# A macaron encoder layer in split fp32: longer leads at three boundaries, and operand places on one offset

## The chip, the cores and the metric

One Trainium2 chip, one of its cores. The metric is device time of one execution in microseconds: 1952.46 us before the change (median of 3 runs, 1952.25 to 1954.24).

## The reference

One encoder layer on x of 256 tokens by 2048 channels, float32, with three blocks, each behind a norm that is modulated by nine vectors made from c:

```python
mod = silu(c) @ w_ada + b_ada            # 2048 -> 9 * 2048
h = rms_norm(x, ffn1_pre_g) * (1 + sc1) + sh1
f = (silu(h @ w_gate) * (h @ w_up)) @ w_down        # 2048 -> 5632 -> 2048
x = x + 0.5 * g1 * rms_norm(f, ffn1_post_g)
h = rms_norm(x, mix_pre_g) * (1 + sc2) + sh2
q, k, v, c_val, c_gate = split(h @ w_in)            # 2048 -> 5120
attn = 8 heads, rotary, three dilated windows
u = silu(layer_norm(depthwise_conv31(c_val * sigmoid(c_gate))))
x = x + g2 * rms_norm(concat(rms_norm(attn), rms_norm(u)) @ w_out, mix_post_g)
# then a second FFN like the first, with sh3, sc3, g3
```

## The kernel before

**Matmuls.** The 256 tokens are two halves t of 128 partitions. A product of a 128x128 block of the transposed activations (stationary) and 128x512 weights (moving) is computed from split operands: both sides are held as a rounded part (hi) and a rest (lo), and L316 to L318 add hi*hi, hi*lo and lo*hi into one PSUM bank per half. A Group (L294) is one 512-column block of a product over all its K tiles; it goes by chunks of CH = 2 K tiles. `wchunk` (L280) loads a chunk on the sync queue into one of 7 `raw` buffers, casts it on ACT to `hi` (L290) and subtracts on DVE to `lo` (L291); hi and lo have 4 buffers each. A chunk is 12 matmuls: 2 K tiles, 3 products, 2 halves. Six PSUM banks hold three groups.

**in_step** (L320) loads several chunks, then issues the products of half 0 for all of them, then those of half 1, then one `tick` for each. `group` (L329) takes `head` chunks in one step, then single chunks, then `tail` chunks in one step. With TAIL = 4 at the last group of a block, half 0 is complete 24 matmuls before half 1; with HEAD = 4 the next block begins with half 0 of four chunks.

**Boundaries.** `next_norm` (L409) follows a block: `post_add` of half 0 (norm of f, add to x, sum of squares), `pre_norm` (L360) of half 0 for the first JF = 4 K tiles, `post_add` of half 1, and the rest. `pre_norm` scales x by the norm (DVE), transposes two K tiles (TensorE), applies A and B of the modulation (ACT), and splits into hi and lo (ACT, DVE).

**Modulation.** `mod_sum` (L169) loads w_ada in half-MB blocks into the same `raw` buffers and sums it times silu(c) per partition on DVE (L191); `mod_cols` transposes the sums and adds them up over partitions on ACT. These run as lanes: generators that `tick` steps at a rate per chunk.

**Stages.** `ffn_start` (L465) computes the first six 512-column blocks of gate and up (12 groups) K stage by K stage, since the modulation of the next K tiles is still being made: STAGES1 has four stages of 4 K tiles, STAGES2 has 4, 6 and 6. At the start of the kernel all of stage 0's modulation (16 ada blocks, `first`, L550) precedes the first product. `begin2` (L568) opens FFN 2 with two groups in step. The lane of stage s + 1 is paced so that it ends two chunks before the stage does.

**Places.** Activations live in named places of the work pool (`slot`, L249): `ah`/`al` 0 to 5, `hh`/`hl` 0 to 3, `fs`, `gs`, `ac`; 4096 bytes per partition each, `ah5` and `al5` 4576 (SLOT = 4 * 286 elements). Within a pool tiles follow one another in the order of their first use. By the sizes of what stands before them, the hi/lo buffers start 64 bytes past a multiple of 256, and the places of h at a multiple of 256.

The order within an engine is set by a scheduler when the program is built; program order gives the priority.

Of the kernel before, what the change touches and what calls it, by code (L numbers as in the profile page):

```python
# [9 lines left out]
F32 = mybir.dt.float32  # L10
# [6 lines left out]
P = 128  # L17
# [15 lines left out]
CH = 2  # L33
MW = 1024

HEAD = 4
TAIL = 4  # L40
# [10 lines left out]

RAW = 7
HILO = 4
SLOT = 4 * (S + 2 * PAD)

STAGES1 = ((0, 4), (4, 8), (8, 12), (12, 16))
STAGES2 = ((0, 4), (4, 10), (10, 16))


@with_exitstack  # L60
def encoder_layer(ctx, tc, a, consts, out):
# [215 lines left out]
            return self.lo[k // 4][:, k % 4:k % 4 + n, :]  # L277


    def wchunk(w, r0, kt, cols, name):  # L280

        raw = wpool.tile([P, CH, BLK], F32, tag="raw", bufs=RAW, name=f"raw_{name}")
        hi = wpool.tile([P, CH, BLK], F32R, tag="hi", name=f"hi_{name}")
        lo = wpool.tile([P, CH, BLK], F32R, tag="lo", name=f"lo_{name}")
        r, h, l = raw[:, :kt, :], hi[:, :kt, :], lo[:, :kt, :]
        n = BLK // len(cols)
        for m, n0 in enumerate(cols):
            nc.sync.dma_start(r[:, :, m * n:(m + 1) * n],
                              w[r0:r0 + kt * P, n0:n0 + n].rearrange("(j p) n -> p j n", p=P))
        nc.scalar.copy(h, r)  # L290
        nc.vector.tensor_tensor(l, r, f32(h), op=ALU.subtract)  # L291
        return h, l

    class Group:  # L294
# [6 lines left out]
            self.first, self.last, self.kx = first, last, kx  # L301
            self.chunks = -(-nk // CH)

        def load(self, c):
            kt = min(CH, self.nk - c * CH)
            return wchunk(self.w, (self.k0 + c * CH) * P, kt, self.cols, f"{self.name}_{c}")

        def products(self, c, t, hl):
            ts = slice(t * P, (t + 1) * P)
# [10 lines left out]
    def in_step(work):  # L320

        hls = [g.load(c) for g, c in work]
# [6 lines left out]
    def group(*args, head=0, tail=0, **kw):  # L329

        g = Group(*args, **kw)
        head = min(head, g.chunks - tail)
        mid = range(head, g.chunks - tail)
        for cs in (range(head), *([c] for c in mid), range(g.chunks - tail, g.chunks)):
            in_step([(g, c) for c in cs])
# [72 lines left out]

    def next_norm(f, ssp, A, B, j1, i):  # L409


        hT = Parts(f"h{i}", "h", range(4))
        jh = min(HEAD * CH, j1)
        rs = [post_add(f, post_rstd(ssp, i, 0), i, 0)]
        pre_norm(hT, rs, A, B, 0, JF, i, 0, 1)
        rs.append(post_add(f, post_rstd(ssp, i, 1), i, 1))
        pre_norm(hT, rs, A, B, JF, jh, i, 0, 1)
        pre_norm(hT, rs, A, B, 0, jh, i, 1, 2)
        pre_norm(hT, rs, A, B, jh, j1, i)
        return hT, rs  # L420


    def act_out(aT, i, gs, pu, name):
# [26 lines left out]
    def ffn_down(f, aT, wd, ba, bb, th, G, ssp, i):  # L450
        for db in range(4):
            pd = mm_ps(f"pd{i}_{th}_{db}")
            group(pd, aT, wd, ba * 4, (bb - ba) * 4, db * BLK, f"d{i}_{th}_{db}",
                  tail=TAIL if th == 1 and db == 3 else 0)
            for t in range(NT):
# [4 lines left out]
                if th == 1:  # L460
                    post_block(f, ssp, G, t, db)

    ROUNDS = ((0, 6, (0, 1, 2, 3, 4, 5)), (6, 11, (0, 1, 2, 3, 5)))

# [78 lines left out]
    def ffn1_mods(s):  # L543
        return stage_mods(0, 1, "ffn1_pre_g", A1, B1, *STAGES1[s])
# [328 lines left out]
    drain(conv_entry)  # L873
    drain(mods)
    r2 = rc["conv"]
    for db in range(4):
        po = mm_ps(f"pc{db}")
        group(po, mT, w_out, 8, 8, db * BLK, f"oc{db}", kx=8, tail=TAIL if db == 3 else 0)
        for t in range(NT):
            nc.vector.scalar_tensor_tensor(f[db][:, t, :], po[t], r2[:, t:t + 1],  # L880
                                           f[db][:, t, :], op0=ALU.mult, op1=ALU.add)
            post_block(f, ssp, G2, t, db)


    hT, rs = next_norm(f, ssp, A3, B3, STAGES2[0][1], 3)
# [66 lines left out]
```

## Time and profile before

| | us |
|---|---|
| median of 3 runs | 1952.46 |
| profiled execution | 1953.91 |
| its span, first to last instruction | 1952.1 |
| TensorE busy | 1872.6 (96%) |
| DVE busy | 1474.1 (76%) |
| ACT busy | 928.3 (48%) |
| DMA queue q1, share of 16 engines | 76.1% |
| mean granted TensorE clock | 0.989 |

A row of a timeline has the start, the duration, the engine, the line, the operation with output<-inputs, the shape and a count (x8: eight merged), and in brackets the engine's idle time before it with what ended it. Matmuls overlap: the distance of starts is what one costs, not its duration. In a table of waits stand the total, the count and the longest. A window's row has each engine's busy time, then the granted clock, the DMA share and the rate.

### The profile page before, as it was taken

What the parts mean: (1) busy time and instruction counts of PE and PEld (TensorE: products, weight loads), DVE (VectorE), ACT (ScalarE), POOL (GpSimd) and SP (SyncE); (2) the same over time, 40 slices, a digit from 0 to 9 for tenths busy, and PEclk for the clock granted to TensorE, in tenths of its full rate; (3) what the DMA queues carried; (4) which work ended last, traced back from release to release, by engine and by line L of the source; (5) the groups of instructions that cost most, each with busy time, mean ns of one, the idle gap of its engine ahead of it and who ended that gap; (6) DMA issues with size and microseconds to landing.
All of it is one profiled execution on the core that took longest, in us unless ns stands there. A gap on an engine that the chain in (4) does not pass through costs nothing.

```text
span 1952.1 us, 23783 instructions
## 1 busy us (share of the span) xinstructions
PE 1872.6 (96%) x8358; PEld 1527.1 (78%) x8358; DVE 1474.1 (76%) x1824; ACT 928.3 (48%) x1428; POOL 66.0 (3%) x99
## 2 busy tenths in 40 slices
PE   2999999999999999899999988999999999999997
PEld 1888877888888888688888776687888888888886
DVE  6789999787777776689997777897786556545455
ACT  3554355444444444644456655534444443444442
POOL 2000000000000000000100000000000000000000
PEclk9999999999999999899999999999999999999999
DMA  9989978999999898357555767897777777666653
GB/s 344 310 297 311 323 253 283 348 340 328 314 321 316 317 318 292 109 184 224 173 165 161 239 214 258 301 341 254 226 247 244 244 253 248 195 185 191 206 191 101
DMA packets 250392, 496.29 MB, mean 254 GB/s; under 512 B 17209, under 2 KB 42625, under 8 KB 250272
## 3 DMA queue, kind: packets, MB, share of 16 engines
q1 hardware_dynamic: 247888, 491.38, 76.1%
q0 software_dynamic: 2208, 3.32, 0.5%
q8 instruction: 65, 1.06, 0.2%
q14 instruction: 55, 0.45, 0.1%
q10 hardware_dynamic: 176, 0.07, 0.0%
HBM read 492.58 MB, written 2.12 MB: 253 GB/s over the span
## 4 chain that ended last, share of the span: by engine, by line
PE 88%; DVE 5%; DMA 3%; ACT 2%; issue 2%; POOL 0%; DVEq 0%; POOLq 0%; ACTq 0%; SPq 0%
PE pd_t L318 8%; PE pd_t L317 8%; PE pd_t L316 8%; PE pg_t L317 8%; PE pg_t L318 8%; PE pg_t L316 8%; PE pu_t L318 8%; PE pu_t L317 8%; PE pu_t L316 7%; PE pc_t L316 2%; PE pc_t L318 2%; PE pc_t L317 2%; DVE acc L191 2%; DMA ada<-in_w_ada 1%; PE pa L384 1%
## 5 line engine op out<-in xcount | busy, mean ns | idle before, releaser
L191 DVE SCALAR_TENSOR_TENSOR acc<-ada,cact,acc 128x512 f32<-128x512 f32 (+2 forms) x448 | 384.9, 897 | 12.8 <-DMA acc<-in_b_ada 8.4
L291 DVE TENSOR_TENSOR lo_d<-raw_d,hi_d 128x1024 fp32r<-128x1024 f32 x176 | 215.3, 1225 | 157.6 <-ACT hi_d L290 156.9
L290 ACT CAST hi_d<-raw_d 128x1024 fp32r<-128x1024 f32 x176 | 185.2, 1052 | 261.2 <-PE pd_t L318 181.5
L290 ACT CAST hi_g<-raw_g 128x1024 fp32r<-128x1024 f32 x176 | 185.0, 1052 | 247.2 <-PE pg_t L318 121.0
L291 DVE TENSOR_TENSOR lo_g<-raw_g,hi_g 128x1024 fp32r<-128x1024 f32 x176 | 214.4, 1222 | 105.0 <-ACT hi_g L290 104.8
L291 DVE TENSOR_TENSOR lo_u<-raw_u,hi_u 128x1024 fp32r<-128x1024 f32 x176 | 213.9, 1222 | 104.7 <-ACT hi_u L290 104.4
L290 ACT CAST hi_u<-raw_u 128x1024 fp32r<-128x1024 f32 x176 | 184.8, 1052 | 214.0 <-PE pu_t L318 94.5
L318 PE MATMUL pd_t<-hi_d,a_0l 128*128 128x512 f32 x384 | 151.2, 394 | 0.0
L317 PE MATMUL pd_t<-lo_d,a_0h 128*128 128x512 f32 x384 | 150.5, 392 | 0.0
L316 PE MATMUL pd_t<-hi_d,a_0h 128*128 128x512 f32 x384 | 150.4, 392 | 0.0
L316 PE MATMUL pg_t<-hi_g,h3h 128*128 128x512 f32 x352 | 140.4, 401 | 5.3 <-ACT hi_g L290 4.2
L316 PE MATMUL pu_t<-hi_u,h3h 128*128 128x512 f32 x352 | 139.8, 400 | 2.9 <-ACT hi_u L290 2.9
L317 PE MATMUL pu_t<-lo_u,h3h 128*128 128x512 f32 x352 | 140.0, 398 | 1.7 <-DVE lo_u L291 1.6
L317 PE MATMUL pg_t<-lo_g,h3h 128*128 128x512 f32 x352 | 139.4, 396 | 1.7 <-DVE lo_g L291 1.7
L316 PE MATMUL pg_t<-hi_g,h1h 128*128 128x512 f32 x352 | 139.4, 398 | 1.0 <-ACT hi_g L290 1.0
L318 PE MATMUL pu_t<-hi_u,h3l 128*128 128x512 f32 x352 | 139.7, 397 | 0.0
L317 PE MATMUL pg_t<-lo_g,h1h 128*128 128x512 f32 x352 | 138.7, 394 | 0.8 <-DVE lo_g L291 0.8
L318 PE MATMUL pg_t<-hi_g,h3l 128*128 128x512 f32 x352 | 139.3, 396 | 0.0
L316 PE MATMUL pu_t<-hi_u,h1h 128*128 128x512 f32 x352 | 138.8, 396 | 0.0
L318 PE MATMUL pu_t<-hi_u,h1l 128*128 128x512 f32 x352 | 138.6, 394 | 0.0
L318 PE MATMUL pg_t<-hi_g,h1l 128*128 128x512 f32 x352 | 138.6, 395 | 0.0
L317 PE MATMUL pu_t<-lo_u,h1h 128*128 128x512 f32 x352 | 137.8, 392 | 0.1
(259 smaller groups left out, 3572.1 us busy)
## 6 DMA issues: line engine op xcount, KB each, us to landing
ada<-in_w_ada SPq DMA_DIRECT2D x288, 512.0 KB, 5.3
raw_g<-in_ffn_w_gate SPq DMA_DIRECT2D x176, 512.0 KB, 4.7
raw_u<-in_ffn_w_up SPq DMA_DIRECT2D x176, 512.0 KB, 4.7
raw_d<-in_ffn_w_down SPq DMA_DIRECT2D x176, 512.0 KB, 5.7
raw_c<-in_w_in SPq DMA_DIRECT2D x64, 256.0 KB, 3.1
raw_q<-in_w_in SPq DMA_DIRECT2D x16, 512.0 KB, 4.4
raw_k<-in_w_in SPq DMA_DIRECT2D x16, 512.0 KB, 4.5
raw_v<-in_w_in SPq DMA_DIRECT2D x16, 512.0 KB, 4.2
```

Of the source, the lines that this page charges most:

```text
L191: tc.keep_in_program_order(nc.vector.scalar_tensor_tensor(acc, w[:, j, :], cact[:, j0 + j:j0 + j + 1], acc, op0=ALU.mult, op1=ALU.add))
L290: nc.scalar.copy(h, r)
L291: nc.vector.tensor_tensor(l, r, f32(h), op=ALU.subtract)
L316: nc.tensor.matmul(o, xh, h, start=self.first and k == 0, stop=False)
L317: nc.tensor.matmul(o, xh, l, start=False, stop=False)
L318: nc.tensor.matmul(o, xl, h, start=False, stop=self.last and k == self.nk - 1)
L384: nc.tensor.transpose(ps[:, jj * S + t * P:jj * S + (t + 1) * P], src[:, t, jj * P:(jj + 1) * P], ident)
```

## The change

- The tail of both FFNs becomes 7 chunks in step (TAIL1); `wchunk` can put hi and lo into named places instead of the pools, and three of the seven use TAIL_AT1. `ffn_down` returns the last eviction as a function of the half, which `next_norm` (or the end) calls half by half.
- The mixing block's first group takes all its 8 chunks in one step; four of them are loaded before `next_norm`, into ah0 to al3.
- The end of mixing takes its last two column blocks (8 chunks) in one step, four of them in places; FFN 2 begins with three groups (6 chunks) in one step, four of them loaded before `next_norm`.
- FFN 1 begins with the modulation of two K tiles (EARLY); three groups take their first chunk, the modulation of the next two K tiles follows, then the three second chunks.
- The number of chunks that are ahead, which paces the lane of the next stage, is 6 in both FFNs (0 and 4 before).
- SLOT is rounded up to 1152 elements, and a 64-byte tile `gap` is placed ahead of h.

```diff
-HEAD = 4
-TAIL = 4
+TAIL1 = 7
+TAIL_AT1 = (("hh2", "hl2"), ("hh3", "hl3"), ("gs", "ac"))
+HEAD1 = 8
+HEAD_AT1 = (("ah0", "al0"), ("ah1", "al1"), ("ah2", "al2"), ("ah3", "al3"))
+HEAD_AT2 = TAIL_AT2 = (("ah0", "ah1"), ("ah2", "ah3"), ("al2", "al3"), ("ah5", "al5"))
-SLOT = 4 * (S + 2 * PAD)
+SLOT = -(-4 * (S + 2 * PAD) // 64) * 64
+EARLY = 2
...
-    def wchunk(w, r0, kt, cols, name):
+    def wchunk(w, r0, kt, cols, name, at=None):
         raw = wpool.tile([P, CH, BLK], F32, tag="raw", bufs=RAW, name=f"raw_{name}")
+        if at is None:
+            hi = wpool.tile([P, CH, BLK], F32R, tag="hi", name=f"hi_{name}")
+            lo = wpool.tile([P, CH, BLK], F32R, tag="lo", name=f"lo_{name}")
+        else:
+            hi = slot(at[0], [P, CH, BLK], f"hi_{name}", F32R)
+            lo = slot(at[1], [P, CH, BLK], f"lo_{name}", F32R)
...
+    def load_all(work, places=()):
+        return [g.load(c, places[n] if n < len(places) else None) for n, (g, c) in enumerate(work)]
+
+    def in_step(work, places=(), hls=None):
+        if hls is None:
+            hls = load_all(work, places)
...
-    def next_norm(f, ssp, A, B, j1, i):
-        hT = Parts(f"h{i}", "h", range(4))
-        jh = min(HEAD * CH, j1)
+    def next_norm(hT, f, ssp, A, B, j1, i, evict):
+        evict(0)
         rs = [post_add(f, post_rstd(ssp, i, 0), i, 0)]
         pre_norm(hT, rs, A, B, 0, JF, i, 0, 1)
+        evict(1)
         rs.append(post_add(f, post_rstd(ssp, i, 1), i, 1))
-        pre_norm(hT, rs, A, B, JF, jh, i, 0, 1)
-        pre_norm(hT, rs, A, B, 0, jh, i, 1, 2)
-        pre_norm(hT, rs, A, B, jh, j1, i)
-        return hT, rs
+        pre_norm(hT, rs, A, B, JF, j1, i, 0, 1)
+        pre_norm(hT, rs, A, B, 0, j1, i, 1, 2)
+        return rs
...
-    first = ffn1_mods(0)
-    for n in range(4 * STAGES1[0][1]):
+    first = stage_mods(0, 1, "ffn1_pre_g", A1, B1, 0, EARLY)
+    for n in range(4 * EARLY):
...
+    nc.vector.memset(work.tile([P, 16], F32, name="gap"), 0.0)
     hT = Parts("h1", "h", range(4))
-    pre_norm(hT, rs, A1, B1, *STAGES1[0], "1_0")
+    pre_norm(hT, rs, A1, B1, 0, EARLY, "1_0")
+
+    def begin1(open_group, run, order):
+        k1 = STAGES1[0][1]
+        gs = {}
+        rest = stage_mods(0, 1, "ffn1_pre_g", A1, B1, EARLY, k1)
+        for w, b in order[:3]:
+            gs[w, b] = open_group(w, b, 0, 0, k1, mm_ps(f"p{w}1_{b}_0"))
+        for g in gs.values():
+            in_step([(g, 0)])
+        for _ in rest:
+            pass
+        pre_norm(hT, rs, A1, B1, EARLY, k1, "1_0b")
+        for g in gs.values():
+            in_step([(g, 1)])
+        return {k: (g.ps, k1) for k, g in gs.items()}, 2 * len(gs)
 
     def begin2(open_group, run, order):
-        gs, k1 = {}, STAGES2[0][1]
-        for w, b in order[:2]:
-            ps = mm_ps(f"p{w}2_{b}_0")
-            gs[w, b] = open_group(w, b, 0, 0, k1, ps)
-        in_step([(g, c) for g in gs.values() for c in range(g.chunks)])
-        return {k: (g.ps, k1) for k, g in gs.items()}, k1
+        in_step(ahead2, hls=hls2 + load_all(ahead2[4:]))
+        return {k: (g.ps, STAGES2[0][1]) for k, g in heads2.items()}, len(ahead2)
...
-    hT, rs = next_norm(f, ssp, A2, B2, NK, 2)
+    ps_c0 = mm_ps("pc0")
+    c0 = Group(ps_c0, hT, a["w_in"], 0, NK, (3 * AW, 3 * AW + CW), "c0")
+    ahead = [(c0, c) for c in range(HEAD1)]
+    hls = load_all(ahead[:4], HEAD_AT1)
+    rs = next_norm(hT, f, ssp, A2, B2, NK, 2, evict)
+    in_step(ahead, hls=hls + load_all(ahead[4:]))
...
-        group(po, mT, w_out, 8, 8, db * BLK, f"oc{db}", kx=8, tail=TAIL if db == 3 else 0)
...
+    both = [conv_group(db) for db in (2, 3)]
+    in_step([(g, c) for g in both for c in range(g.chunks)], TAIL_AT2)
+
+    def evict(t):
+        for db in (2, 3):
+            evict_c(db, t)
...
+    heads2 = {}
+    for w, b in (("g", 0), ("u", 0), ("g", 1)):
+        heads2[w, b] = Group(mm_ps(f"p{w}2_{b}_0"), hT, a["ffn2_w_gate" if w == "g" else "ffn2_w_up"], 0,
+                             STAGES2[0][1], b * BLK, f"{w}2_{b}_0_0")
+    ahead2 = [(g, c) for g in heads2.values() for c in range(g.chunks)]
+    hls2 = load_all(ahead2[:4], HEAD_AT2)
+    rs = next_norm(hT, f, ssp, A3, B3, STAGES2[0][1], 3, evict)
...
     for t in range(NT):
+        evict(t)
         r = post_rstd(ssp, 4, t)
```

## Rows read from the trace of the kernel before

**Rows 1.** The page: busy times of the engines, and costliest groups of two lines.

```profile
PE 1872.6 (96%) x8358; PEld 1527.1 (78%) x8358; DVE 1474.1 (76%) x1824; ACT 928.3 (48%) x1428; POOL 66.0 (3%) x99
...
L290 ACT CAST hi_g<-raw_g 128x1024 fp32r<-128x1024 f32 x176 | 185.0, 1052 | 247.2 <-PE pg_t L318 121.0
L291 DVE TENSOR_TENSOR lo_g<-raw_g,hi_g 128x1024 fp32r<-128x1024 f32 x176 | 214.4, 1222 | 105.0 <-ACT hi_g L290 104.8
```

**Rows 2.** Waits of TensorE over the span (total, count, longest).

```profile
PE psc L206 <- ACT hi_g L290: 20.4, 1, 20.4
PE pst L371 <- DVE xn L368: 14.8, 2, 7.5
```

**Rows 3.** Timeline of the start (start, duration, what).

```profile
20.64 2.08 DVE L191 SCALAR_TENSOR_TENSOR acc<-ada,cact,acc 128x512 f32<-128x512 f32 x3 [0.69 <-DMA ada<-in_w_ada]
...
22.13 0.63 ACT L339 ACTIVATE jx<-x 128x512 f32<-128x512 f32 x1
...
35.24 1.94 PE L206 MATMUL psc<-ident,acc 128*128 128x128 f32 x8 [20.39 <-ACT hi_g L290]
...
42.63 0.79 PE L316 MATMUL pg_t<-hi_g,h1h 128*128 128x512 f32 x1
```

**Rows 4.** Window before the first product (busy times, clock, DMA share, GB/s).

```profile
0.00:42.60 42.60, 4.97 (x19) 3.54 (x19) 28.09 (x45) 14.23 (x45) 12.57 (x26) 1.00 0.99 353
```

**Rows 5.** Groups of line 191 by form, 9 to 36 us and 1230 to 1256 us.

```profile
L191 DVE SCALAR_TENSOR_TENSOR acc<-ada,cact,acc 128x512 f32<-128x512 f32 x32 | 21.8, 745 | 10.7 <-DMA acc<-in_b_ada 8.4 <-DMA ada<-in_w_ada 2.2
...
L191 DVE SCALAR_TENSOR_TENSOR acc<-ada,cact,acc 128x256 f32<-128x256 f32 x32 | 13.0, 477 | 0.0
```

**Rows 6.** Timeline of the boundary FFN 1 to mixing.

```profile
793.78 0.40 PE L316 MATMUL pd_t<-hi_d,a_1h 128*128 128x512 f32 x1
...
807.57 1.16 ACT L376 ACTIVATE hf<-pst,B,A 128x128 f32<-128x128 f32 x3 [2.88 <-PE pst L371]
808.61 0.41 ACT L357 CAST h2h<-hf 128x256 fp32r<-128x256 f32 x1
...
809.07 0.79 PE L316 MATMUL pc_t<-hi_c,h2h 128*128 128x512 f32 x1 [1.12 <-ACT h2h L357]
```

**Rows 7.** Window after that boundary.

```profile
810.00:815.00 5.00, 5.00 (x15) 3.93 (x15) 1.59 (x8) 4.09 (x13) 0.70 (x1) 0.50 0.01 3
```

**Rows 8.** Timeline of the boundary mixing to FFN 2.

```profile
1160.88 0.39 PE L316 MATMUL pc_t<-hi_oc,mh 128*128 128x512 f32 x1
...
1176.26 0.80 PE L316 MATMUL pg_t<-hi_g,h3h 128*128 128x512 f32 x1 [1.11 <-ACT h3h L357]
```

**Rows 9.** Windows of FFN 2's first stage.

```profile
1176.26:1256.49 80.23, 73.80 (x298) 56.98 (x299) 63.30 (x101) 43.53 (x86) 4.42 (x7) 0.93 0.81 282
...
1180.00:1190.00 10.00, 10.00 (x46) 8.08 (x45) 5.30 (x11) 6.83 (x12) 0.54 (x1) 0.97 0.07 10
```

**Rows 10.** Waits of the sync queue, 1176 to 1262 us.

```profile
SPq L288 <- DVE lo_g L291: 21.0, 9, 15.1
```

**Rows 11.** Timeline of TensorE: starts of matmuls in three places.

```profile
70.10 0.40 PE L316 MATMUL pg_t<-hi_g,h1h 128*128 128x512 f32 x1
...
73.60 0.40 PE L316 MATMUL pu_t<-hi_u,h1h 128*128 128x512 f32 x1
...
640.04 0.39 PE L316 MATMUL pu_t<-hi_u,h1h 128*128 128x512 f32 x1
...
643.25 0.39 PE L318 MATMUL pg_t<-hi_g,h1l 128*128 128x512 f32 x1
643.47 0.39 PE L316 MATMUL pg_t<-hi_g,h1h 128*128 128x512 f32 x1
...
645.53 0.39 PE L316 MATMUL pg_t<-hi_g,h1h 128*128 128x512 f32 x1
...
1535.47 0.40 PE L316 MATMUL pd_t<-hi_d,a_0h 128*128 128x512 f32 x1
...
1540.38 0.40 PE L316 MATMUL pd_t<-hi_d,a_0h 128*128 128x512 f32 x1
```

More of the change, by code (lines that the diff above doesn't have):

```diff
@@ L277, in l @@
             return self.lo[k // 4][:, k % 4:k % 4 + n, :]
-    def wchunk(w, r0, kt, cols, name):
+    def wchunk(w, r0, kt, cols, name, at=None):
         raw = wpool.tile([P, CH, BLK], F32, tag="raw", bufs=RAW, name=f"raw_{name}")
-        hi = wpool.tile([P, CH, BLK], F32R, tag="hi", name=f"hi_{name}")
-        lo = wpool.tile([P, CH, BLK], F32R, tag="lo", name=f"lo_{name}")
+        if at is None:
[4 more added lines that the diff above has]
+            lo = slot(at[1], [P, CH, BLK], f"lo_{name}", F32R)
         r, h, l = raw[:, :kt, :], hi[:, :kt, :], lo[:, :kt, :]
@@ L302, in __init__, with load @@
             self.chunks = -(-nk // CH)
-        def load(self, c):
+        def load(self, c, at=None):
             kt = min(CH, self.nk - c * CH)
-            return wchunk(self.w, (self.k0 + c * CH) * P, kt, self.cols, f"{self.name}_{c}")
+            return wchunk(self.w, (self.k0 + c * CH) * P, kt, self.cols, f"{self.name}_{c}", at)
         def products(self, c, t, hl):
@@ L318, in products @@
                 nc.tensor.matmul(o, xl, h, start=False, stop=self.last and k == self.nk - 1)
-    def in_step(work):
-        hls = [g.load(c) for g, c in work]
+    def load_all(work, places=()):
[3 more added lines that the diff above has]
+            hls = load_all(work, places)
         for t in range(NT):
@@ L327, in in_step, with group @@
             tick()
-    def group(*args, head=0, tail=0, **kw):
+    def group(*args, tail=0, places=(), **kw):
         g = Group(*args, **kw)
[L332 to L335, printed above, removed]
+        for c in range(g.chunks - tail):
+            in_step([(g, c)])
+        if tail:
+            in_step([(g, c) for c in range(g.chunks - tail, g.chunks)], places)
     def square_sum(src, dst, name):
@@ L453, in ffn_down, with evict @@
             group(pd, aT, wd, ba * 4, (bb - ba) * 4, db * BLK, f"d{i}_{th}_{db}",
-                  tail=TAIL if th == 1 and db == 3 else 0)
-            for t in range(NT):
+                  tail=TAIL1 if th == 1 and db == 3 else 0, places=TAIL_AT1)
+            def evict(t, db=db, pd=pd):
                 if th == 0:
@@ L459, in ffn_down @@
                     nc.vector.tensor_tensor(f[db][:, t, :], pd[t], f[db][:, t, :], op=ALU.add)
-                if th == 1:
                     post_block(f, ssp, G, t, db)
+            if th == 1 and db == 3:
+                return evict
+            for t in range(NT):
+                evict(t)
     ROUNDS = ((0, 6, (0, 1, 2, 3, 4, 5)), (6, 11, (0, 1, 2, 3, 5)))
@@ L528, in ffn_rest @@
             G = gate() if th == 1 else None
-            ffn_down(f, aT, wd, ba, bb, th, G, ssp, i)
-        return f, ssp
+            evict = ffn_down(f, aT, wd, ba, bb, th, G, ssp, i)
+        return f, ssp, evict
     A1, B1 = affine_tiles(1)
@@ L587, in encoder_layer @@
                    lambda s: pre_norm(hT, rs, A1, B1, *STAGES1[s], f"1_{s}"),
-                   (later_mods(), LRATE))
-    f, ssp = ffn_rest(hT, aT, a["ffn1_w_gate"], a["ffn1_w_up"], a["ffn1_w_down"],
-                      lambda: gate_tile(g1, 1), 1)
+                   (later_mods(), LRATE), begin1)
+    f, ssp, evict = ffn_rest(hT, aT, a["ffn1_w_gate"], a["ffn1_w_up"], a["ffn1_w_down"],
+                             lambda: gate_tile(g1, 1), 1)
     drain_all()
-    hT, rs = next_norm(f, ssp, A2, B2, NK, 2)
+    QC = BLK // 2
+    hT = Parts("h2", "h", range(4))
+    ps_c0 = mm_ps("pc0")
[4 more added lines that the diff above has]
+    in_step(ahead, hls=hls + load_all(ahead[4:]))
     w_in = a["w_in"]
@@ L616, in encoder_layer, with in_group @@
         nc.gpsimd.memset(u[:, :, PAD + S:], 0.0)
-    def in_group(o, name, head=0):
+    def in_group(o, name):
         ps = mm_ps(f"p{name}")
-        group(ps, hT, w_in, 0, NK, o, name, head=head)
+        group(ps, hT, w_in, 0, NK, o, name)
         return ps
@@ L830, in encoder_layer @@
     rc = {}
-    QC = BLK // 2
     conv_entry = None
     for g in range(CW // QC):
-        ps = in_group((3 * AW + g * QC, 3 * AW + CW + g * QC), f"c{g}", head=HEAD if g == 0 else 0)
+        ps = in_group((3 * AW + g * QC, 3 * AW + CW + g * QC), f"c{g}") if g else ps_c0
         gs = gs_tile(f"c{g}")
@@ L875, in encoder_layer, with conv_group, evict_c @@
     r2 = rc["conv"]
-    for db in range(4):
-        po = mm_ps(f"pc{db}")
-        group(po, mT, w_out, 8, 8, db * BLK, f"oc{db}", kx=8, tail=TAIL if db == 3 else 0)
-        for t in range(NT):
[L880 to L885, printed above, removed]
+    pcs = [None] * 4
+    def conv_group(db):
+        pcs[db] = mm_ps(f"pc{db}")
+        return Group(pcs[db], mT, w_out, 8, 8, db * BLK, f"oc{db}", kx=8)
+    def evict_c(db, t):
+        nc.vector.scalar_tensor_tensor(f[db][:, t, :], pcs[db][t], r2[:, t:t + 1],
+                                       f[db][:, t, :], op0=ALU.mult, op1=ALU.add)
+        post_block(f, ssp, G2, t, db)
+    for db in range(2):
+        g = conv_group(db)
+        for c in range(g.chunks):
+            in_step([(g, c)])
+        for t in range(NT):
+            evict_c(db, t)
[3 more added lines that the diff above has]
+        for db in (2, 3):
+            evict_c(db, t)
+    hT = Parts("h3", "h", range(4))
+    heads2 = {}
[5 more added lines that the diff above has]
+    rs = next_norm(hT, f, ssp, A3, B3, STAGES2[0][1], 3, evict)
     aT = ffn_start(hT, a["ffn2_w_gate"], a["ffn2_w_up"], 2, STAGES2, ffn2_mods,
@@ L888, in encoder_layer @@
                    (mod_gate(8, "ffn2_post_g", 0.5, g3), 0.3), begin2)
-    f, ssp = ffn_rest(hT, aT, a["ffn2_w_gate"], a["ffn2_w_up"], a["ffn2_w_down"],
-                      lambda: gate_tile(g3, 3), 2)
+    f, ssp, evict = ffn_rest(hT, aT, a["ffn2_w_gate"], a["ffn2_w_up"], a["ffn2_w_down"],
+                             lambda: gate_tile(g3, 3), 2)
     for t in range(NT):
+        evict(t)
         r = post_rstd(ssp, 4, t)
```

## The prediction

> **What bounds the kernel now.** The page's busy table comes first: TensorE is busy 1872.6 of the 1952.1 us of the span, the next engine 76% [rows 1]. So time is won only where TensorE stands still or runs at half clock, or where its matmuls come closer together. The table of waits shows the standstills: one of 20.4 us before the first modulation is transposed, and two of about 7.4 us (14.8 together) for a normalised x [rows 2]. The timeline places them: the first product of the kernel starts at 42.63 us [rows 3], and the two others end at the boundaries FFN 1 to mixing and mixing to FFN 2, whose first products start at 809.07 and 1176.26 [rows 6, 8]. The windows add what follows such a standstill, a stretch at a granted clock of 0.50, the 1.2 GHz level [rows 7], and a fourth place: FFN 2's first stage, 24 chunks of 12 matmuls, lasts 80.2 us at a mean clock of 0.93 [rows 9], while 288 matmuls at the usual 0.2288 us (24 starts in 5.49 us) need 66 us [rows 11].
>
> **Start.** Today 16 ada blocks of half a MB and x must land before the first product, with DMA at 0.99 share and 353 GB/s [rows 4]. Now 8 blocks must; 4.2 of 10.5 MB go behind. The eighth block is summed from 20.64 us on, and the last square of x is at 22.13 [rows 3]. DVE's 32 sums become half as wide: 13.0 us for 32 instead of 21.8 [rows 5]. The last eight (3.2 us) can begin at 20.64, so the transposes of the modulation move from 35.24 to about 24. From there to the first product took 7.4 us; with two K tiles instead of four I take 5: first product at 29. Three groups give 36 matmuls, 8.2 us of work, done by 40 at the latest.
> The other half of the modulation queues behind three weight blocks on the sync queue: 22 us + 1.6 MB + 4.2 MB at 353 GB/s = 38.5, last sums 3 us, then the same 5 us: the second K tiles start at 46.7. TensorE stands still for some 7 us there, so it restarts at half clock as it does at 42.63 today; that price cancels. What counts is 42.6 against 46.7 - 8.2 = 38.5: **gain 4.1 us**; 8 if the second half is not late, -1 (a loss) if DVE, which now splits three weight blocks meanwhile, delays it 5 us.
> The price behind: stage 0's next ada blocks are spread over 16 chunks instead of 22, 1.0 instead of 0.73 per chunk. Per chunk DVE then has one split of 1.2 [rows 1] and two sums of 0.68 [rows 5], 2.6 of the 2.75 us of 12 matmuls; DMA 1.05 MB per 2.75 us, 381 GB/s, over the 353 of the start. The queue is ahead at that point, which covers most: **loss 1 us**, 0 to 5.
>
> **FFN 1 to mixing.** Token half 0 is complete when half 1's first product starts, 793.78, and the chain (evict, square, power, add to x, square, power, scale, transpose, affine, cast) reaches the next group's first product at 809.07, 15.3 us later [rows 6]. Half 1's 24 matmuls cover 5.5 of it. With seven chunks in the tail 42 matmuls cover 9.6: 4.1 more. Against it: the first four weight blocks of the next group now stand ahead of the chain in program order, and three of their places (ah1 to ah3) come free only while half 1 proceeds; a cast of 1.05 or a split of 1.2 us [rows 1] can stand before a link of the chain. That is 0 to 3.6 us; I take one split, 1.2. The head of eight chunks then asks for all 16 K tiles of half 0 in one go: per pair of K tiles ACT needs two affines of 0.39 and a cast of 0.41, 1.2 us [rows 6], against 1.37 us of matmuls and some 0.25 of transposes, but four casts and four squares of half 1 come between: 17 us of ACT against 13 of TensorE, of which the half clock of the restart hides some 3. I take 0.4 of loss; 0 to 4. **Gain 2.5 us** (-3.5 to 4.1). Some 7 us without products remain, so I let the clock fall as now.
>
> **Mixing to FFN 2.** The same: 1160.88 to 1176.26 is 15.4 us [rows 8], covered by 5.5. Two column blocks of four chunks in step cover 48 x 0.2288 = 11.0: 5.5 more. The chain grows by a second eviction and gate product (two 128x512 passes, nearest row the sum of 0.68 [rows 5]: 1.4 us) and by a split (0 to 3.6, I take 1.0). **Gain 3.1 us** (0.5 to 5.5).
>
> **FFN 2's first stage.** It wants 48 blocks, 25.2 MB; the DMA share is 0.07 from 1180 to 1190 [rows 9], because the sync queue stood 15.1 us for a raw buffer that a split frees [rows 10], and the splits wait for hi/lo buffers that the four head chunks hold. Four of six head chunks now lie in work places, so up to four more blocks (2.1 MB, 6 us of the queue) move before it stalls, and the head gives 16.5 us of work instead of 11. But the ada blocks come 1.5 per chunk instead of 1.33, on a DVE that is already busy 63.3 of 80.2 us [rows 9]. The stage can't go below 66, so the ends are 0 and 14; nearer to the blocks: **gain 4 us**.
>
> **Operand places.** By the code the hi/lo pools start 64 bytes past a multiple of 256, the work places at a multiple of 256, and `al5`, 4576 bytes after `ah5`, 32 bytes past a multiple of 64. In the K tiles of slot 5 matmuls start 233.8 ns apart (21 starts in 4.91 us), else 228.8 [rows 11]. They are 4 K tiles x 3 products x 2 halves x 4 column blocks x 2 rounds x 2 FFNs = 384: **1.9 us gained** by the rounding. The 64-byte `gap` moves all stationary operands to the pools' offset. No row shows such a pair. The nearest: 233.3 ns, which also stood in FFN 1's first stage with even places (15 starts in 3.50 us), and single steps of 0.22 to 0.23 us (643.25 to 643.47) [rows 11], say 225; over 7680 matmuls -29 to +35 us. Offset 0 is the row nearest to 64, both multiples of 64: I take 0.
> The Trainium skill (SBUF — State Buffer, in the section on Door 1, its box on cachelines) speaks of lines of 16 bytes. By it an offset of 32 is as good as 0 or 64, the rounding gives nothing and the sum would be 1.9 us smaller; the rows of slot 5 disagree. The skill's TensorE: Matmul & The Clock Gate (Back-to-back issue gap) gives 518 cycles for 512 columns, an estimate of 215.8 ns; by it the spacing has room, but no row here reaches it.
>
> **The end** doesn't move: half 0's output chain is hidden behind half 1's products already, and half 1's starts after the last product in both.
>
> **Sum.** -4.1 + 1.0 - 2.5 - 3.1 - 4.0 - 1.9 = -14.6. The profiled execution took 1953.9 (span 1952.1 and 1.8 around it): 1939.3. The median of the runs shown is 1.45 lower: **1938 us**.
>
> **Rivals.**
> A. The leads are eaten: the second modulation half is late (gain 0), the splits stand in both chains in full and ACT holds the head up (gain 0 and 0.5), the stage gains nothing because DVE is late next. Left are 1.9 + 0.5 - 1.0: about 1951. For it: casts and splits are placed before the chain; against: the standstills are long, and the cover is a count of matmuls.
> B. The slower side: the common offset puts all matmuls at 233.3 ns. (7680 - 384 - 288 that are there already) x 4.5 ns = 31.5; without the rounding's 1.9: 1938 + 33.4 = 1971. For it: 32 bytes on one operand of three did this, and the first stage shows that it can last without any; against: stationary places at a multiple of 256 ran at 228.8 in all later stages. It decides from 2 ns per matmul on.
> C. The common offset closes the spacing to 225: 7296 x 3.8 = 28 us less: 1910. For it: single steps of that size recur; against: longer ones follow each, and three together are what holds.
> D. The change doesn't do what it says: the scheduler sets the casts so late that the longer tails cover nothing new. That ends in A's numbers and is counted there.
>
> **How the numbers follow.** Forecast 0.62 (its own range 1927 to 1949), A 0.14, B 0.12, C 0.12. A measurement of this kernel tells about 0.2%, 3.9 us, from no change. A lies half in faster, the rest in same but for 0.01: faster 0.62 + 0.12 + 0.07 = 0.81, same 0.06, slower 0.13. The range leaves out B and most of C: 1919 to 1954.
>
> **What would show it.** First product near 29 us and a standstill of about 7 us before the second K tiles; the waits of the transposes at the boundaries down from 7.4 to 3 to 5 us; FFN 2's first stage at 70 to 77 us; slot 5's matmuls 228.8 ns apart like the others. It is wrong if the first stage's second K tiles start after 50 us, if a boundary's wait stays above 7 us, or if the spacing in FFN 1's later stages is not 228.8.

## The result: 1923.7 us, twice the forecast gain

| | before | after |
|---|---|---|
| median, 4 runs each, side by side | 1952.54 | 1923.72 |
| lowest to highest | 1952.25 to 1954.24 | 1921.65 to 1925.33 |
| profiled execution (span) | 1953.91 (1952.1) | 1925.33 (1923.5) |

The ratio is 0.985 (95% interval 0.9833 to 0.9867): 28.8 us less. The forecast was 1938, 14.5 us less. The direction is right and the time lies in the range, but the size is half of what came. The profiled execution of after was the slowest of its four runs; where traces are compared below, 28.6 us stand between them.

In the profile after, line numbers are higher: the three matmul lines are L326 to L328, the sums of the modulation L196, the cast and the split of weights L300 and L301, the transposes of x L385. First the page's busy table [rows 1 before]:

```profile
PE 1854.6 (96%) x8358; PEld 1524.1 (79%) x8358; DVE 1478.0 (77%) x1862; ACT 929.7 (48%) x1440; POOL 70.1 (4%) x102
```

TensorE has the same 8358 instructions and is busy 18 us less. So not only standstills went: the instructions themselves came closer together, or ran less at half clock. The timeline of TensorE shows the first: here are the first and the last of 24 matmuls of slot 5, then two starts of FFN 2's upward products that are 48 starts apart [rows 11 before]:

```profile
1510.59 0.39 PE L326 MATMUL pd_t<-hi_d,a_0h 128*128 128x512 f32 x1
...
1515.80 0.39 PE L328 MATMUL pd_t<-hi_d,a_0l 128*128 128x512 f32 x1
...
1640.07 0.39 PE L326 MATMUL pg_t<-hi_g,h3h 128*128 128x512 f32 x1
...
1650.95 0.39 PE L326 MATMUL pu_t<-hi_u,h3h 128*128 128x512 f32 x1
```

10.88 us for 48 are 226.7 ns each, where before had 228.8; slot 5 is no exception any more (23 steps in 5.21 us, 226.5 ns; 233.8 before; a row's 0.01 us is 0.4 ns here).

The table of TensorE's waits, its first seven rows (total, times, longest) [rows 2 before]:

```profile
PE psc L211 <- DVE acc L196: 12.3, 3, 9.5
PE pst L385 <- DVE xn L382: 9.6, 3, 4.7
PE ps_prm L159 <- DMA rows<-in_ffn_post_g: 8.2, 1, 8.2
PE ps_c L143 <- DMA ident<-const_ident: 6.5, 1, 6.5
PE pg_t L326 <- ACT h1h L371: 5.4, 2, 3.3
PE pu_t L327 <- DVE lo_u L301: 4.9, 2, 4.4
PE pg_t L327 <- DVE lo_g L301: 3.2, 4, 2.1
```

The wait for the modulation fell from 20.4 to 12.3, that for a normalised x from 14.8 to 9.6; a new one of 3.3 us for `h1h` belongs to the second K tiles. The timeline of the start and of the two boundaries, TensorE and one DVE group [rows 3, 6 and 8 before]:

```profile
24.95 1.08 PE L211 MATMUL psc<-ident,acc 128*128 128x128 f32 x4 [9.55 <-DVE acc L196]
...
31.38 0.80 PE L326 MATMUL pg_t<-hi_g,h1h 128*128 128x512 f32 x1 [2.13 <-ACT h1h L371]
...
32.59 12.75 DVE L196 SCALAR_TENSOR_TENSOR acc<-ada,cact,acc 128x256 f32<-128x256 f32 x32
...
42.21 0.39 PE L328 MATMUL pg_t<-hi_g,h1l 128*128 128x512 f32 x1
45.09 0.74 PE L211 MATMUL psc<-ident,acc 128*128 128x128 f32 x4 [2.50 <-DVE acc L196]
...
50.33 0.80 PE L326 MATMUL pg_t<-hi_g,h1h 128*128 128x512 f32 x1 [3.31 <-ACT h1h L371]
...
789.77 0.39 PE L328 MATMUL pd_t<-hi_d,a_1l 128*128 128x512 f32 x1
794.88 1.02 PE L385 MATMUL pst<-ident,xn 128*128 128x128 f32 x4 [4.71 <-DVE xn L382]
...
797.01 0.79 PE L326 MATMUL pc_t<-hi_c,h2h 128*128 128x512 f32 x1
...
1153.45 0.39 PE L328 MATMUL pc_t<-hi_oc,ml 128*128 128x512 f32 x1
1158.27 1.11 PE L385 MATMUL pst<-ident,xn 128*128 128x128 f32 x4 [4.43 <-DVE xn L382]
1160.49 0.79 PE L326 MATMUL pg_t<-hi_g,h3h 128*128 128x512 f32 x1 [1.11 <-ACT h3h L371]
```

The first product starts 11.2 us earlier, the second K tiles 7.7 us later than all four did before. Each boundary keeps a wait of 4.4 to 4.7 us. Windows after the first boundary (first row) and of FFN 2's first and second stages [rows 7 and 9 before]:

```profile
797.00:802.00 5.00, 5.00 (x13) 3.74 (x13) 5.00 (x10) 4.76 (x15) 0.00 (x0) 0.52 0.29 100
...
1160.49:1240.91 80.42, 74.40 (x316) 59.21 (x316) 65.90 (x108) 43.95 (x87) 6.59 (x8) 0.94 0.83 281
1241.13:1345.91 104.78, 102.71 (x456) 84.20 (x455) 93.27 (x134) 48.64 (x75) 2.89 (x4) 0.98 0.91 305
```

The clock still falls to its 1.2 GHz level behind the boundary (0.52). From the first product of each stretch to that of the next (for the boundaries, from the last product of one block to the first of the next), the two traces compare so, us. The last column is the run with the places alone (see the experiments), which has the new places and the old leads:

| stretch | before | after | change | of it spacing | places alone |
|---|---|---|---|---|---|
| to the first product of FFN 1's second stage | 114.33 | 111.56 | -2.8 | -1.8 (288 x 6.2 ns) | 111.74 |
| rest of FFN 1 | 684.77 | 678.21 | -6.6 | -6.3 (2880 x 2.2), slot 5 -0.9 | 678.67 |
| boundary FFN 1 to mixing | 9.97 | 7.24 | -2.7 | | 10.05 |
| mixing | 357.07 | 356.44 | -0.6 | -3.0 (1344 x 2.2) | 356.40 |
| boundary mixing to FFN 2 | 10.12 | 7.04 | -3.1 | | 10.17 |
| FFN 2, first stage | 83.69 | 80.64 | -3.1 | -0.6 | 83.52 |
| FFN 2, second stage | 109.19 | 105.01 | -4.2 | -1.0 | 106.99 |
| rest of FFN 2 | 572.63 | 567.21 | -5.4 | -5.4 (2448 x 2.2), slot 5 -0.9 | 567.21 |

The changes sum to 28.4 us. The column of spacing is worked out from counts; some 16 us of the change is spacing (mixing keeps 0.6 of its 3.0), where the forecast had 1.9. Against the last column, the leads took 0.2 us from the start, 2.8 and 3.1 from the boundaries, 2.9 and 2.0 from FFN 2's first two stages, and 0.5 from the rest of FFN 1.

### The profile page after: what moved, and what is told of

It reads as the page before. It is cut to its first block, busy times and chain, and to the rows that moved or that the text cites. A ratio compares the mean times of both kernels' runs of the same rounds, so it can differ in the third digit from the quotient of the medians.

```text
span 1923.5 us, 23827 instructions
## 1 busy us (share of the span) xinstructions
PE 1854.6 (96%) x8358; PEld 1524.1 (79%) x8358; DVE 1478.0 (77%) x1862; ACT 929.7 (48%) x1440; POOL 70.1 (4%) x102
## 4 chain that ended last, share of the span: by engine, by line
PE 84%; DVE 7%; ACT 3%; DMA 3%; issue 2%; POOL 0%; DVEq 0%; POOLq 0%; SPq 0%; ACTq 0%
PE pd_t L328 8%; PE pd_t L326 8%; PE pd_t L327 8%; PE pg_t L327 8%; PE pg_t L328 7%; PE pg_t L326 7%; PE pu_t L327 7%; PE pu_t L328 7%; PE pu_t L326 7%; DVE acc L196 3%; PE pc_t L328 2%; PE pc_t L327 2%; PE pc_t L326 2%; PE pa L398 1%; PE pv_t L328 1%
## 5 line engine op out<-in xcount | busy, mean ns | idle before, releaser
L196 DVE SCALAR_TENSOR_TENSOR acc<-ada,cact,acc 128x512 f32<-128x512 f32 (+2 forms) x480 | 388.9, 852 | 11.9 <-DMA acc<-in_b_ada 9.7
L301 DVE TENSOR_TENSOR lo_d<-raw_d,hi_d 128x1024 fp32r<-128x1024 f32 x176 | 214.7, 1224 | 135.7 <-ACT hi_d L300 135.0
L300 ACT CAST hi_g<-raw_g 128x1024 fp32r<-128x1024 f32 x176 | 185.4, 1053 | 241.7 <-PE pg_t L328 110.1
L300 ACT CAST hi_d<-raw_d 128x1024 fp32r<-128x1024 f32 x176 | 184.9, 1054 | 238.5 <-PE pd_t L328 169.5
L301 DVE TENSOR_TENSOR lo_g<-raw_g,hi_g 128x1024 fp32r<-128x1024 f32 x176 | 214.4, 1222 | 109.4 <-ACT hi_g L300 109.1
L300 ACT CAST hi_u<-raw_u 128x1024 fp32r<-128x1024 f32 x176 | 185.0, 1053 | 218.7 <-PE pu_t L328 93.7
L301 DVE TENSOR_TENSOR lo_u<-raw_u,hi_u 128x1024 fp32r<-128x1024 f32 x176 | 214.0, 1222 | 97.1 <-ACT hi_u L300 96.7
L326 PE MATMUL pd_t<-hi_d,a_0h 128*128 128x512 f32 x384 | 149.9, 391 | 0.0
L328 PE MATMUL pd_t<-hi_d,a_0l 128*128 128x512 f32 x384 | 149.5, 389 | 0.0
L326 PE MATMUL pg_t<-hi_g,h1h 128*128 128x512 f32 x352 | 139.2, 398 | 6.1 <-ACT h1h L371 5.4
L326 PE MATMUL pg_t<-hi_g,h3h 128*128 128x512 f32 x352 | 139.6, 398 | 1.3 <-ACT h3h L371 1.3
L326 PE MATMUL pu_t<-hi_u,h3h 128*128 128x512 f32 x352 | 138.7, 395 | 0.7 <-ACT hi_u L300 0.7
L328 PE MATMUL pg_t<-hi_g,h3l 128*128 128x512 f32 x352 | 138.5, 394 | 0.0
L328 PE MATMUL pu_t<-hi_u,h3l 128*128 128x512 f32 x352 | 138.1, 392 | 0.0
L326 PE MATMUL pu_t<-hi_u,h1h 128*128 128x512 f32 x352 | 138.1, 394 | 0.0
L328 PE MATMUL pg_t<-hi_g,h1l 128*128 128x512 f32 x352 | 137.9, 393 | 0.0
L328 PE MATMUL pu_t<-hi_u,h1l 128*128 128x512 f32 x352 | 137.3, 390 | 0.0
```

What stands on the lines that cost most here:

```text
L196: tc.keep_in_program_order(nc.vector.scalar_tensor_tensor(acc, w[:, j, :], cact[:, j0 + j:j0 + j + 1], acc, op0=ALU.mult, op1=ALU.add))
L326: nc.tensor.matmul(o, xh, h, start=self.first and k == 0, stop=False)
```

## The experiments

All are the kernel after, or before where it says so, with one edit. The spacing given is the mean distance of neighbouring matmul starts at full clock over the whole trace: 229.4 ns in before (7336 pairs), 227.2 in after (7334).

**The gap taken away.**

```diff
-    nc.vector.memset(work.tile([P, 16], F32, name="gap"), 0.0)
```

> The changed kernel without the 64-byte tile ahead of h; the rounding of SLOT and all leads stay. Stationary operands at a multiple of 256 again, moving ones 64 past it. Theory P (the common offset closed the spacing of matmuls from 228.8 to 226.7 ns and gave about 15 of the 29 us): spacing back to 228.8, time 1936 to 1941. Rival L (the leads gave nearly all, and the spacing closed through them or through the rounding): spacing stays 226.7, time 1922 to 1926.

Measured 1937.84 (1937.12 to 1938.13), ratio 0.9924 (0.991 to 0.9939); spacing 229.0 ns. Its trace, TensorE, 48 starts apart:

```profile
1644.05 0.39 PE L327 MATMUL pg_t<-lo_g,h3h 128*128 128x512 f32 x1
...
1655.04 0.39 PE L327 MATMUL pg_t<-lo_g,h3h 128*128 128x512 f32 x1
```

10.99 us, 228.9 ns each: the pace of before. The 64 bytes are worth 1937.84 - 1923.72 = 14.1 us; 7680 x (228.99 - 227.16) ns = 14.1. Without them the kernel takes the forecast time, so the sum of all the other terms was right; the terms one by one were not (see the leads below).

**The places alone**, in the kernel before:

```diff
-SLOT = 4 * (S + 2 * PAD)
+SLOT = -(-4 * (S + 2 * PAD) // 64) * 64
...
+    nc.vector.memset(work.tile([P, 16], F32, name="gap"), 0.0)
```

> The kernel before with the 64-byte tile and the rounding of SLOT alone, no lead changed. Theory P: spacing 226.7 in every stage, time 1935 to 1937 (7680 matmuls x 2.2 ns = 17 us less than 1952.5). Rival L: spacing 228.8, only the 1.9 us of slot 5 gone: 1950 to 1951.

Measured 1937.48 (1935.54 to 1938.93), ratio 0.9923 (0.9907 to 0.994); spacing 227.2. Its trace, TensorE, 48 starts apart:

```profile
1645.55 0.39 PE L317 MATMUL pg_t<-lo_g,h3h 128*128 128x512 f32 x1
...
1656.45 0.39 PE L317 MATMUL pg_t<-lo_g,h3h 128*128 128x512 f32 x1
```

10.90 us, 227.1 ns each. Places alone give 15.1 us and the leads, as what is left to after, 13.8; without an edit of the order in the program the closer spacing came whole.

**All operands at a multiple of 256.** 192 bytes ahead of everything else shift both sides alike:

```diff
+    nc.vector.memset(keep.tile([P, 48], F32, name="pad"), 0.0)
```

> The changed kernel with a 192-byte tile more at the end of the first pool, so that moving and stationary operands both lie at a multiple of 256 instead of 64 past it. Theory P1 (it is the equality of the two offsets that counts): spacing 226.7, time as the changed kernel, 1924. Rival P2 (it is the stationary operand's 64 that counts): 228.8, 1939. Rival P3 (what counts is each operand's place in a 128-byte unit, both at its start now): below 226.7, time under 1915.

A single run: 1921.59. Its trace, TensorE, 48 starts apart:

```profile
1640.18 0.39 PE L328 MATMUL pg_t<-hi_g,h3l 128*128 128x512 f32 x1
...
1651.06 0.39 PE L328 MATMUL pu_t<-hi_u,h3l 128*128 128x512 f32 x1
```

226.7 ns. It is not the place 64 of the stationary operand that pays: with the stationary operand at 0 the pace is 228.9 when the moving one lies at 64, and 226.7 when it lies at 0 too.

**Stationary places at 192, 128 and 96, moving at 64.** Three kernels, which differ in the length of the gap (48, 32 and 24 elements for 16):

```diff
-    nc.vector.memset(work.tile([P, 16], F32, name="gap"), 0.0)
+    nc.vector.memset(work.tile([P, 48], F32, name="gap"), 0.0)
```

> The changed kernel with 192 bytes ahead of h instead of 64: stationary operands 192 past a multiple of 256, moving ones in the pools still 64 past it, so they differ by 128. P1 (equal offsets modulo 256): spacing 228.8 or more, about 1939. P2 (an odd multiple of 64 for the stationary operand, or a difference that is a multiple of 128): 226.7, about 1924.

> The changed kernel with 128 bytes ahead of h: stationary operands 128 past a multiple of 256, moving ones 64 past it in the pools. By the runs so far the spacing hangs on the difference of the two offsets modulo 256: 0 gives 226.7 ns, 192 gave 228.8, 128 gave 232.6. This is the difference 64. If only equality is fast: 228.8 to 232, 1938 to 1962. If a second difference is as fast as 0: 1924.

> The changed kernel with 96 bytes ahead of h: all stationary operands 32 bytes past the moving ones of the pools. Slot 5 alone, one product of three, paid 13.5 ns per three matmuls for such a difference. If each product pays alike: 226.7 + 13.5 = 240 ns, about 2025 us. If the price is one per three matmuls however many differ: 231.2, about 1958.

One run each: 1959.69, 1964.59 and 1961.25; spacing 232.6, 233.2 and 233.1 ns. Timelines of TensorE 48 starts apart, for 192, 128 and 96 in this order:

```profile
1640.14 0.39 PE L328 MATMUL pu_t<-hi_u,h3l 128*128 128x512 f32 x1
...
1651.30 0.39 PE L328 MATMUL pu_t<-hi_u,h3l 128*128 128x512 f32 x1
```

```profile
1640.17 0.39 PE L328 MATMUL pu_t<-hi_u,h3l 128*128 128x512 f32 x1
...
1651.37 0.39 PE L328 MATMUL pu_t<-hi_u,h3l 128*128 128x512 f32 x1
```

```profile
1640.15 0.40 PE L327 MATMUL pu_t<-lo_u,h3h 128*128 128x512 f32 x1
...
1651.35 0.40 PE L327 MATMUL pu_t<-lo_u,h3h 128*128 128x512 f32 x1
```

11.16, 11.20 and 11.20 us: 232.5, 233.3 and 233.3 ns. So not any offset costs alike. By the distance from the moving to the stationary operand, modulo 256, the steady pace is 226.7 at 0, 228.9 at 192 (the kernel before), 232.5 at 128, 233.3 at 64 and at 32. Four of these five were run with the moving operand at 64 only, so that the distance alone counts rests on the two equal places. The distance 64 is slower than the 232 ns that bounded what was expected of it. For 96 both guesses missed: 231.2 ns, a price paid once per three matmuls, is too low and 240 too high. The nanoseconds of that trace have steps of 231 or 232 and 235 in turn, so every step is longer than the 226 and 227 of after, not one of three. In the kernel before, steps of 226, 229 and 232 ns follow one another in a cycle, whose longest step stands behind hi*hi in some stretches and behind lo*hi in others. In slot 5 of before, where one of three stationary operands lay at a distance of 160, all three steps are longer, 230 to 236. Why the distance matters none of these runs tells.

**The rounding undone**, the gap kept:

```diff
-SLOT = -(-4 * (S + 2 * PAD) // 64) * 64
+SLOT = 4 * (S + 2 * PAD)
```

> The changed kernel with SLOT at 1144 elements, so that the lo part of slot 5 alone starts 32 bytes past a multiple of 64 (32 against the 64 of the rest). The prediction gave the rounding 1.9 us against a spacing of 228.8. Theory: 233.3 against 226.7 ns for 384 matmuls, 2.5 us: 1926.2. Rival: a difference of 32 bytes costs nothing in itself, and slot 5 was slow for another reason: 1923.7.

Measured 1926.02 (1925.38 to 1927.76), ratio 0.9868 (0.9851 to 0.9884): 2.3 us over after. Its trace, the first and the last of the 24 matmuls of slot 5 that stand for those shown of after:

```profile
1512.30 0.39 PE L326 MATMUL pd_t<-hi_d,a_0h 128*128 128x512 f32 x1
...
1517.62 0.39 PE L328 MATMUL pd_t<-hi_d,a_0l 128*128 128x512 f32 x1
```

5.32 us for 23 steps, 231.3 ns against 226.5. The four stretches of downward products are 0.42 to 0.46 us longer each, 1.74 together. The term of 1.9 us holds in size, though the two pairs of places are not the same: here the lo part leaves the distance 0, in the kernel before it left 192.

**The start undone.** All four K tiles of modulation again before the first product:

```diff
-EARLY = 2
+EARLY = 4
...
-                   (later_mods(), LRATE), begin1)
+                   (later_mods(), LRATE))
```

> The changed kernel with the old start: modulation of four K tiles before the first product, no groups begun early, the next lane paced over 22 chunks. The prediction gave this step 4.1 - 1.0 us: it expects 1926 to 1928. From the end of FFN 1's first stage in the two traces (114.3 before, 111.6 after, of which 0.6 to 1.9 is the closer spacing) I now expect less: 1924.5 to 1926.

Measured 1927.51 (1925.71 to 1929.55), ratio 0.9877 (0.9862 to 0.9891): 3.8 us over after by the medians, but its profiled execution took 1926.91, only 1.6 over that of after, and its second stage starts at 112.96 against 111.56, 1.4 later. What the medians show beyond that has no place in the trace. The run with the places alone has the old start too, and there the second stage starts at 111.74, 0.2 after. So the start is worth 0.2 to 1.4 us.

**The lead of FFN 1 to mixing undone.** Tail and head of four, weights loaded behind the norm:

```diff
-TAIL1 = 7
-TAIL_AT1 = (("hh2", "hl2"), ("hh3", "hl3"), ("gs", "ac"))
-HEAD1 = 8
+TAIL1 = 4
+TAIL_AT1 = ()
+HEAD1 = 4
...
-    hls = load_all(ahead[:4], HEAD_AT1)
-    rs = next_norm(hT, f, ssp, A2, B2, NK, 2, evict)
-    in_step(ahead, hls=hls + load_all(ahead[4:]))
+    rs = next_norm(hT, f, ssp, A2, B2, NK, 2, evict, HEAD1 * CH)
+    in_step(ahead)
+    for c in range(HEAD1, 8):
+        in_step([(c0, c)])
```

> The changed kernel with the old boundary FFN 1 to mixing: tail of 4, head of 4, no chunks loaded ahead of the chain. The prediction gave it 2.5 us (1926.2). From the traces the boundary went from 10.0 to 7.2 us between the last and the first product: 1926 to 1927. Rival: the closer products bring forward a wait later in mixing (the stretch from q, k, v to the end of mixing took 259.5 us after and 258.8 before although spacing should have saved 2), then undoing costs under 1 us.

Measured 1927.63 (1926.16 to 1929.72), ratio 0.9878 (0.9863 to 0.9893): 3.9 by the medians, 0.8 between the profiled executions. In the trace the boundary is 9.71 us long against 7.24, but the first products of mixing (its 384 for the convolution) then take 95.44 against 96.68, 1.2 less. That the long head costs those 1.2 is not shown: with the places alone, which has the old head too, they take 97.24.

**The lead of mixing to FFN 2 undone.** One column block after the other at the end, a tail of four; two groups begun, loaded behind the norm:

```diff
-    both = [conv_group(db) for db in (2, 3)]
-    in_step([(g, c) for g in both for c in range(g.chunks)], TAIL_AT2)
...
-    for w, b in (("g", 0), ("u", 0), ("g", 1)):
+    for w, b in (("g", 0), ("u", 0)):
...
-    hls2 = load_all(ahead2[:4], HEAD_AT2)
```

> The changed kernel with the old boundary mixing to FFN 2: column blocks one by one with a tail of 4, FFN 2 begun with two groups that are loaded after the chain. The prediction gave 3.1 us for the boundary and 4 us for the first stage: 1930.8. From the traces: 3.1 at the boundary, 2.4 in the first stage and 3.2 in the second one, 1931 to 1933. Rival: the stages gained by chance of the queue, not by the lead; then about 1927.

Measured 1932.35 (1930.74 to 1933.86), ratio 0.9901 (0.9886 to 0.9916): 8.6 by the medians, 7.5 between the profiled executions. Windows of FFN 2's first and second stages:

```profile
1162.82:1246.20 83.38, 76.76 (x316) 59.28 (x316) 67.27 (x110) 46.72 (x91) 4.42 (x7) 0.93 0.81 282
1246.42:1353.40 106.98, 102.85 (x456) 84.16 (x455) 93.76 (x134) 48.55 (x74) 2.88 (x4) 0.98 0.88 299
```

2.8 us of the boundary (9.82 against 7.04), 3.0 of the first stage (83.61 against 80.64) and 2.2 of the second (107.21 against 105.01) stand in the trace. Mixing is 1.6 shorter (354.82 against 356.44), but not by the edit: the run without the rounding, whose mixing is that of after, has 355.05.

**A longer tail, and with it a short head.** The first: nine chunks in step at the end of both FFNs, five of them in places. The second has the same and a head of four.

```diff
-TAIL1 = 7
-TAIL_AT1 = (("hh2", "hl2"), ("hh3", "hl3"), ("gs", "ac"))
+TAIL1 = 9
+TAIL_AT1 = (("hh0", "hl0"), ("hh1", "hl1"), ("hh2", "hl2"), ("hh3", "hl3"), ("gs", "ac"))
```

> The changed kernel with a tail of nine chunks at both FFNs' ends, five of them in places (hh0 to hh3, gs). Half 1 covers 54 x 0.2267 = 12.2 us of the chain instead of 9.5. If the boundary is the chain less its cover, 2.7 us less: 1921. If the casts for the next head, whose places come free later now, hold the chain: no gain, 1923.7 or more.

> The same tail of nine, and mixing's first group with a head of four chunks (loaded ahead of the chain into their places) and the other four one by one, so that ACT has fewer casts before the first half is through. The run with the old boundary took 95.4 us for the input columns of the convolution against 96.7 with the head of eight: 1.2 us less than the tail of nine alone, 1919.8. Rival: that difference came from the colder start of the longer head and goes with the shorter standstill; then as the tail of nine.

The first: 1921.32 (1921.15 to 1923.34), ratio 0.9841 (0.9827 to 0.9856), 2.4 us under after, the lowest median here; its interval overlaps that of after. The second: 1924.98 (1923.59 to 1926.5), ratio 0.9856 (0.984 to 0.9873). In both the boundary is only 3.2 us long (790.13 to 793.34 and 789.46 to 792.66). The windows that follow it, first of the long head, then of the short:

```profile
793.34:802.00 8.66, 8.26 (x32) 6.35 (x33) 8.22 (x18) 7.86 (x21) 0.58 (x1) 0.80 0.65 207
802.00:820.00 18.00, 17.70 (x86) 13.40 (x85) 9.01 (x24) 13.84 (x36) 0.54 (x1) 1.00 0.09 30
```

```profile
792.66:802.00 9.34, 6.56 (x26) 4.55 (x26) 7.91 (x16) 6.34 (x18) 0.80 (x2) 1.00 0.78 245
802.00:820.00 18.00, 16.69 (x72) 13.29 (x73) 9.19 (x21) 11.66 (x25) 0.40 (x1) 0.81 0.00 1
```

With the short head TensorE is busy 6.56 of 9.34 us, waiting for `h2l` and `hf`, and its clock falls in the window after that (0.81 over 18 us); with the long head it has fallen in the first window (0.80 over 8.66 us) and is whole again in the second. Mixing's first products last 101.53 us against 96.80. The wait that the longer tail took from the boundary came back behind it; the head of eight is what keeps it. The gain of 1.2 us that was expected of the short head did not come.

## Why the prediction was half right

**Operand places: the step that failed.** The prediction wrote "Offset 0 is the row nearest to 64, both multiples of 64: I take 0." It gave each operand's own place the say. The runs show that the place of one relative to the other counts: equal places at 64 (after) and at 0 run alike, and 192 bytes of distance, which the kernel before had everywhere but for the lo part of slot 5, cost 2.2 ns per matmul. The term is -14.1 us, not 0. The prediction's own sign of being wrong, a spacing other than 228.8 in FFN 1's later stages, came true. That the time lies in the range at all is luck: it lies outside the 1927 to 1949 of the forecast, in the part of rival C that the wider range takes in. The range had been drawn from rows at both sides, 225 and 233.3 ns, and both ends were nearly met: rival C's direction came with half its size (226.7, not 225), and rival B's pace of 233.3 is what the kernel runs at with 96 or 128 in place of 64 (its 1971 came out as 1961 to 1965). The row of single steps of 0.22 us, which spoke for C, shows nothing: a step of 226 ns stands in the cycle of 226, 229 and 232 of before and in that of 226 and 227 of after. What could have been drawn from the rows is that only one distance had been seen apart from slot 5, so that "stationary places at a multiple of 256 ran at 228.8 in all later stages" was no evidence that 228.8 is the floor.

**Rounding**: 1.9 forecast, 1.7 in the trace and 2.3 by the medians. An estimate from the lines of 16 bytes that the Trainium skill's SBUF — State Buffer gives in its box on cachelines (section on Door 1) made it 0: 32 bytes cost 231.3 against 226.5 ns here, so the measurement speaks against drawing that from it. The 215.8 ns, an estimate from the 518 cycles that the Trainium skill's TensorE: Matmul & The Clock Gate (Back-to-back issue gap) gives for the isolated gap of a matmul, were reached by no run; the closest pace is 226.7.

**The leads together**: forecast 4.1 - 1.0 + 2.5 + 3.1 + 4.0 = 12.7, measured 13.8 by the run with the places alone. Undone one at a time they give 3.8 + 3.9 + 8.6 = 16.3 by the medians and 1.6 + 0.8 + 7.5 = 9.9 by the profiled executions, so each term is known to some 2 us only, and the sum is the better number. That the sum came so near is in part luck: the start gave some 2 to 3 us less than forecast, and FFN 2's second stage, for which nothing was forecast, gave 2.0.

- Start: first product at 31.4, not 29, and the second K tiles at 50.3, not 46.7; the bound set for "wrong" was 50. The failing part is "last sums 3 us": the timeline has all 32 sums of the second half in one stretch from 32.59 on, 12.75 us, because DVE first did what the first products need. The transposes follow at 45.09 where 41.5 was worked out. The term had this as its low end (DVE delays it, a loss of 1); start and price together were forecast at 3.1 and gave 0.2 to 1.4. The price of 1 behind it doesn't show: from the second K tiles on, the 252 other matmuls take 61.2 us, with the old start all 288 take 69.7, in both some 4 us more than 226.7 ns each.
- FFN 1 to mixing: the boundary gained 2.7 with a wait of 4.7, as forecast (3 to 5). The loss of 0.4 behind it can't be told from the traces: the first products of mixing take 96.68 us with the long head, 95.44 and 97.24 in the two runs with the old one. ACT is busy 4.76 of 5.00 us after the boundary, as "17 us of ACT against 13 of TensorE" had it.
- Mixing to FFN 2: 3.1 forecast, 3.1 in the trace.
- FFN 2's first stage: 80.4 us, not 70 to 77. Here the prediction also misread its row: the window of 80.2 us [rows 9] ends before the stage does, whose last product starts at 1259.72, 83.5 us from its first (the row below). The forecast gain of 4 would have led to some 79.5.

```profile
1176.26:1259.72 83.46, 77.03 (x315) 59.72 (x316) 66.52 (x108) 46.76 (x91) 4.42 (x7) 0.93 0.81 281
```

The longest wait of the sync queue fell from 15.1 to 7.9 us, as the step had it:

```profile
SPq L298 <- DVE lo_g L301: 11.5, 5, 7.9
```

But the head of three groups then waits 4.4 us for a `lo_u` (the row in the table of waits): the splits are late next. Of the 4.0 forecast 2.9 came here, by the run with the places alone, and 2.0 more in the second stage, of which the prediction said nothing: from before to after TensorE's waits there went from 4.0 to 2.1 us and its mean clock from 0.97 to 0.98 (1 us of 109).

**Mixing** kept little of the closer spacing, 0.6 of 3.0 us. In its longest stretch, the products of q, k and v with attention between them, nothing was gained (149.0 us before, 149.1 after), and DVE is busy 144.0 of those 149.1 us; that DVE sets the pace there is likely, but no run changes its work. The first stage of FFN 1 ran at 233.3 ns in before although its operands lay at the same distance as everywhere; in after, without the gap (229.0), without the rounding, with the old start and with the places alone it did not. So the distance alone does not fix the pace in every stretch; what held it there stays open.

## What to carry to other kernels

Where matmuls run back to back, look up the byte offsets of both operands before taking their pace as the floor: one small tile that makes the offsets equal modulo 256 was worth as much here as all the rebuilt leads. A rival whose price is a few ns times every matmul is cheap to test and outweighs careful sums of waits. When a tail is lengthened, look at what the next block's first products wait for: with a short head the whole gain came back as waits of 1 to 2 us and a lower clock.

## What the runs showed of the hardware

For 128x512 matmuls on these operands, the pace followed the distance from moving to stationary operand modulo 256 bytes: 0, 226.7 ns; 192, 228.9 (but 233.3 in one stage of the kernel before); 128, 232.5; 64 and 32, 233.3. It did so in programs that differ in small unused tiles alone, from 1921.6 to 1964.6 us for the whole kernel, three times what all the leads brought. Five distances of one kind of matmul were run, four of them with the moving operand at 64. Within a tile the operands step by multiples of 512 bytes, so a period of 512 in place of 256 was not ruled out. Why the distances differ, and whether other shapes do the same, stays open.
